# GpSimd's inverse square roots of the norms, issued in pieces of two columns

## The chip, the cores and the metric

One Trainium2 chip, of which the kernel uses one core. The metric is device time in microseconds (us) of one execution; less is better. The engines of the core are named as the profile names them: PE (TensorE, with PEld for its weight loads), DVE (VectorE), ACT (ScalarE), POOL (GpSimd), and SP, which issues most DMAs.

## The reference

One layer of a hybrid block on 512 tokens of width 1024, in float32: a norm and one wide projection `z = h @ w_in`, three token mixers fed from `z` (HGRN2, RWKV-7, multi-head latent attention), a gated merge, an output projection, and a gated feed-forward. The change touches the places where an inverse square root is taken:

```python
def rms_norm(x, g):                                   # in and out of both halves, HGRN2's heads, the two MLA ranks
    y = xf * lax.rsqrt(jnp.mean(xf * xf, axis=-1, keepdims=True) + NORM_EPS)
...
kk = heads(k * k_k)                                   # RWKV-7: unit-length keys, 16 heads
kk = kk * lax.rsqrt(jnp.maximum(jnp.sum(kk * kk, axis=-1, keepdims=True), 1e-24))
...
y = ((y - mean) * lax.rsqrt(var + RW_LNX_EPS))        # RWKV-7: norm of each head's output
```

## The kernel before

Tokens or features lie on the 128 partitions. Products that need full precision are made of three passes over operands split into a high and a low part (`mm3`, lines 137 to 139: high by high, low by high, high by low). The wide projections are streamed: `stream` (line 209 on) takes a slab of weights (DMA, then ACT makes the high part at line 205, then DVE the low part at line 132) and issues groups of three matmuls of 512 columns into a PSUM tile named mmD. Everything else of the mixers is interleaved between these groups on PE: the preparation of RWKV's eight pairs of heads (`rwkv_prep`), its chain over eight chunks (`rwkv_chain`), HGRN2's eight heads (`hgrn_head`), and the attention (`mla_low` and what follows). The order on each engine is made by the tile framework's scheduler, which plans by priorities ("lanes") and by its own simulated timeline, so a change in how many instructions an engine gets moves work on all engines.

The dense groups are paced by POOL. After the last matmul of each paced group POOL writes one element (the tile token, line 149, `pace`), and the first matmul of a group waits for the token of the group five places earlier. There are 912 tokens, one for each paced group, all on POOL's queue in order. The streams of the feed-forward are not paced.

POOL also does the powers: `power_mhalf` (line 277) raises a tile of sums to -0.5 by one `tensor_tensor` with `op=pow` against a constant tile filled with -0.5. It is called on these tiles:

- nrs, one column, eight times, and rrs, one column, eight times (`to_fm` and `project`, by way of `rstd`): the norms over the width of 1024.
- rs, eight columns, once for each of RWKV's eight pairs (line 552). Its input ss (line 550) is made by DVE from the sums of squares that four small products (line 547) leave in PSUM. ACT then copies rs broadcast into a tile (line 555, named t), and PE transposes it (line 557).
- hrs, four columns, once for each of HGRN2's eight heads (line 899). ACT reads it column by column (line 901).
- lnr, sixteen columns, four times, once for each two chunks of the chain (line 788). DVE reads it at line 789.
- mrs, eight columns, once (line 1011), from the sums of products at line 1001. DVE reads the first four columns (line 1013), PE the other four, one at a time, as weights (line 1016).

Of the kernel before, what the change touches and what calls it, by code (L numbers as in the profile page):

```python
# [17 lines left out]
ALU = mybir.AluOpType  # L18
# [84 lines left out]
class Kern:  # L103
# [172 lines left out]

    def power_mhalf(self, dst, src):
        p, n = src.shape
        self.nc.gpsimd.tensor_tensor(dst, src, self.mhalf[:p, :n], op=ALU.pow)  # L279

    def vec(self, name, j):
        o = VOFF[name] + j
# [1083 lines left out]
```

## Time and profile before

| what | value |
|---|---|
| time, median of 3 runs | 1403.33 us (1401.97 to 1404.83) |
| time of the profiled execution | 1408.42 us |
| its span, first to last instruction | 1406.6 us |
| mean granted TensorE clock | 0.996 |
| instructions in the span | 27356 |
| PE busy | 1354.8 us (96%) |
| PEld busy | 1103.2 us (78%) |
| DVE busy | 848.3 us (60%) |
| ACT busy | 638.6 us (45%) |
| POOL busy | 190.8 us (14%) |

A busy share is the time in which the engine had an instruction under way. Matmuls overlap in the pipeline, so one matmul's duration is longer than the distance to the next. In a timeline each row has the start, the length of the merged stretch, the engine, the line, the operation, output<-input and the count, and in brackets how long the engine sat idle before it and what ended that wait.

### The profile page before, as it was taken

Reading aid. Unit: us, or ns where it says so; the run is one execution under the profiler, and the core shown is the slowest. Engines: PE = TensorE matmul, PEld = TensorE weight load, DVE = VectorE, ACT = ScalarE, POOL = GpSimd, SP = SyncE. Lnnn points to the kernel's source line nnn. Section 1 sums busy time; section 2 is a strip of 40 time slices with the busy share of each in tenths; the row PEclk is TensorE's granted clock in tenths of the full one; section 3 lists DMA queues with packets and bytes.
Section 4 is the critical chain, followed back from the end, with each engine's and each line's share of the span. In section 5 each row is a group of like instructions: output and inputs, shape, how many; then the busy total and the mean of one; then the engine's idle time right before and its main releaser. Section 6 shows DMA issues by size and latency. Waiting matters only on the chain.

```text
span 1406.6 us, 27356 instructions
## 1 busy us (share of the span) xinstructions
PE 1354.8 (96%) x9664; PEld 1103.2 (78%) x9664; DVE 848.3 (60%) x1756; ACT 638.6 (45%) x1259; POOL 190.8 (14%) x1042
## 2 busy tenths in 40 slices
PE   6999999999999999999999999999999999999998
PEld 5777777777777777888788888877888888888886
DVE  5567797797787784575665576655575344343234
ACT  5554546556556453433665354443354333332222
POOL 2122132131222311242210000001010000000000
PEclk9999999999999999999999999999999999999999
DMA  5565467557755777986464555415544333334233
GB/s 180 149 193 144 129 183 227 178 153 218 213 157 155 242 237 227 356 277 208 137 204 147 157 178 168 130 53 173 198 139 135 98 97 92 102 95 156 97 98 105
DMA packets 196025, 231.62 MB, mean 165 GB/s; under 512 B 42672, under 2 KB 137392, under 8 KB 195888
## 3 DMA queue, kind: packets, MB, share of 16 engines
q1 hardware_dynamic: 194496, 226.72, 52.1%
q10 hardware_dynamic: 1392, 3.15, 0.7%
q8 instruction: 76, 1.25, 0.4%
q14 instruction: 61, 0.50, 0.1%
HBM read 169.65 MB, written 60.16 MB: 163 GB/s over the span
## 4 chain that ended last, share of the span: by engine, by line
PE 82%; DMA 6%; DVE 4%; issue 4%; ACT 3%; POOL 1%; SPq 1%; POOLq 0%; DVEq 0%; ACTq 0%
PE mmD L137 18%; PE mmD L138 17%; PE mmD L139 17%; PE po L137 4%; PE po L139 4%; PE po L138 4%; PE pr L194 1%; DMA wsD<-in_w_in_dram 1%; DMA z<-zst 1%; DMA zr<-z 1%; PE pmo L1138 1%; PE pm L137 1%; PE pm L139 1%; PE pm L138 1%; PE ph L843 1%
## 5 line engine op out<-in xcount | busy, mean ns | idle before, releaser
L137 PE MATMUL mmD<-xH,whD 128*128 128x512 f32 (+1 forms) x1232 | 486.2, 397 | 11.9 <-POOL token L149 5.6
L138 PE MATMUL mmD<-xL,whD 128*128 128x512 f32 (+1 forms) x1232 | 474.2, 386 | 0.0
L139 PE MATMUL mmD<-xH,wlD 128*128 128x512 f32 (+1 forms) x1232 | 469.6, 385 | 0.9 <-DVE wlD L132 0.9
L132 DVE TENSOR_TENSOR wlD<-wsD,whD 128x512 fp32r<-128x512 f32 x384 | 263.2, 687 | 292.0 <-ACT whD L205 276.0
L205 ACT CAST whD<-wsD 128x512 fp32r<-128x512 f32 x384 | 236.7, 618 | 375.8 <-PE mmD L138 244.1
L137 PEld LDWEIGHTS mmD<-xH,whD 128*128 128x128 f32 x1232 | 232.0, 189 | 65.2 <-POOL token L149 8.9
L139 PEld LDWEIGHTS mmD<-xH,wlD 128*128 128x128 f32 x1232 | 232.2, 189 | 48.6 <-DVE wlD L132 2.0
L138 PEld LDWEIGHTS mmD<-xL,whD 128*128 128x128 f32 x1232 | 233.5, 190 | 40.1
L149 POOL MEMSET token<- 1x1 f32 x912 | 82.2, 90 | 675.4 <-PE mmD L139 660.1
L139 PE MATMUL po<-whD,fL 128*128 128x512 f32 x176 | 68.6, 390 | 0.0
L138 PE MATMUL po<-wlD,fH 128*128 128x512 f32 x176 | 68.6, 390 | 0.0
L137 PE MATMUL po<-whD,fH 128*128 128x512 f32 x176 | 61.9, 390 | 0.0
L279 POOL TENSOR_TENSOR rrs<-rtm,mhalf 128x1 f32<-128x1 f32 x8 | 4.4, 551 | 402.3 <-DVE rtm L274 368.7
L646 DVE TENSOR_TENSOR invtmp<-inv 64x30 f32<-64x30 f32 (+14 forms) x120 | 38.7, 322 | 17.7 <-DMA inv<-Ld 16.0
L594 POOL TENSOR_SCALAR BK<-BK,gC 128x128 f32<-128x128 f32 x56 | 47.0, 854 | 11.8 <-PE pr L194 11.8
L237 ACT COPY zst<-mmD 128x512 f32<-128x512 f32 x64 | 37.3, 583 | 14.6 <-PE mmD L139 14.4
L647 DVE TENSOR_TENSOR inv<-inv,invtmp 64x30 f32<-64x30 f32 (+14 forms) x120 | 38.4, 320 | 2.2
L139 PEld LDWEIGHTS po<-whD,fL 128*128 128x128 f32 x176 | 33.0, 188 | 7.0
L138 PEld LDWEIGHTS po<-wlD,fH 128*128 128x128 f32 x176 | 33.0, 188 | 7.0
L137 PEld LDWEIGHTS po<-whD,fH 128*128 128x128 f32 x176 | 33.0, 188 | 7.0
L843 PEld LDWEIGHTS ph<-hq,hk 128*32 128x32 f32 x1536 | 17.6, 111 | 18.0 <-issue 9.6
L1136 ACT COPY mpT<-pmt 128x128 f32<-128x128 f32 (+3 forms) x32 | 13.6, 425 | 38.0 <-PE pmt L1134 37.9
(349 smaller groups left out, 1960.1 us busy)
## 6 DMA issues: line engine op xcount, KB each, us to landing
wsD<-in_w_in_dram SPq DMA_DIRECT2D x176, 256.0 KB, 3.4
wsD<-in_w_ffn_in_dram SPq DMA_DIRECT2D x96, 256.0 KB, 2.8
z<-zst SPq DMA_DIRECT2D x63, 256.0 KB, 3.3
rwd<-G SPq DMA_DIRECT2D x28, 512.0 KB, 5.5
G<-rwd SPq DMA_DIRECT2D x28, 512.0 KB, 6.7
wsD<-in_w_branch_dram SPq DMA_DIRECT2D x48, 256.0 KB, 2.9
wsD<-in_w_ffn_out_dram SPq DMA_DIRECT2D x44, 256.0 KB, 2.6
zr<-z SPq DMA_DIRECT2D x26, 256.0 KB, 3.3
```

Of the source, the lines that this page charges most:

```text
L132: (eng or self.nc.vector).tensor_tensor(dst, src, high.bitcast(F32), op=ALU.subtract)
L137: first = mm(ps, lhsT=lh, rhs=rh, start=start, stop=False)
L138: mm(ps, lhsT=lh, rhs=rl, start=False, stop=False)
L139: return first, mm(ps, lhsT=ll, rhs=rh, start=False, stop=stop)
L149: token = self.nc.gpsimd.memset(self.token, 0.0).ins
L194: last = c()
L205: nc.scalar.copy(h, st)
L237: self.nc.scalar.copy(st[:m], ps)
L594: Pl.tensor_scalar(BK[:, c], BK[:, c], gC[:, c + 1:c + 2], None, op0=ALU.mult)
L646: V.tensor_tensor(tv, cv, rv, op=ALU.mult)
L647: V.tensor_tensor(U[:, :j, j + 1:], U[:, :j, j + 1:], tv, op=ALU.add)
L843: mm(g[b:b + HB, o // P, :], lhsT=k[:, t], rhs=q[:, t], start=True, stop=True)
```

## The change

`power_mhalf` issues one power for each two columns in place of one for the whole tile. Nothing else is edited; lines behind it move by three.

```diff
     def power_mhalf(self, dst, src):
         p, n = src.shape
-        self.nc.gpsimd.tensor_tensor(dst, src, self.mhalf[:p, :n], op=ALU.pow)
+
+        for c in range(0, n, 2):
+            m = slice(c, min(c + 2, n))
+            self.nc.gpsimd.tensor_tensor(dst[:, m], src[:, m], self.mhalf[:p, m], op=ALU.pow)
```

A tile of one column keeps its one instruction. rs and mrs become four instructions each, hrs two, lnr eight. The scheduler's order moves with it on every engine.

On POOL at the fifth pair of RWKV's preparation (lw is the pair's decay tile, rs the powers, token the pacing of the dense groups, BK the scaled keys), before:

```order
L521 MEMSET lw_5663 128x8
L149 MEMSET token 1x1 x8
L279 TENSOR_TENSOR rs_5691<-ss_5689,mhalf 128x8
L149 MEMSET token 1x1 x24
L594 TENSOR_SCALAR BK_5702<-BK_5702,gC_4658 128x128 x4
```

and the same place in the changed kernel:

```order
L524 MEMSET lw_5675 128x8
L149 MEMSET token 1x1 x5
L282 TENSOR_TENSOR rs_5703<-ss_5701,mhalf 128x2 x3
L149 MEMSET token 1x1
L282 TENSOR_TENSOR rs_5703<-ss_5701,mhalf 128x2
L149 MEMSET token 1x1 x31
```

The power is now four instructions, with one token between the third and the fourth. Counted from the start of the queue, 284 tokens stand ahead of the first piece, where 282 stood ahead of the whole power.

On POOL at the end of the chain and the start of the attention (krL is a zeroed half of a tile, mrs the attention's powers, lnr the chain's last powers), before:

```order
L1039 MEMSET krL_10418 64x512
L149 MEMSET token 1x1 x10
L279 TENSOR_TENSOR mrs_10377<-mtm_10376,mhalf 128x8
L279 TENSOR_TENSOR lnr_7451<-lnv_7450,mhalf 128x16
L149 MEMSET token 1x1 x270
```

and in the changed kernel:

```order
L1042 MEMSET krL_10481 64x512
L149 MEMSET token 1x1 x9
L282 TENSOR_TENSOR lnr_7496<-lnv_7495,mhalf 128x2 x8
L282 TENSOR_TENSOR mrs_10437<-mtm_10436,mhalf 128x2 x4
L149 MEMSET token 1x1 x254
```

The two powers have changed places: all eight pieces of lnr stand ahead of mrs, and no token stands between.

On PE at the same place, the products that read mrs (line 1016 before, 1019 now) among the dense groups, before:

```order
L137 MATMUL mmD_4155<-xH_10_111,whD_4181 128x512
L138 MATMUL mmD_4155<-xL_18_119,whD_4181 128x512
L139 MATMUL mmD_4155<-xH_10_111,wlD_4182 128x512
L137 MATMUL mmD_4156<-xH_9_110,whD_4181 128x512
L138 MATMUL mmD_4156<-xL_17_118,whD_4181 128x512
L139 MATMUL mmD_4156<-xH_9_110,wlD_4182 128x512
L1016 MATMUL pm_10385<-cst,mrs_10377 128x128 x4
L1028 MATMUL pm_10398<-cst,msq_10396 128x64 x4
L137 MATMUL mmD_4156<-xH_10_111,whD_4181 128x512
```

and in the changed kernel:

```order
L137 MATMUL mmD_4252<-xH_9_110,whD_4277 128x512
L138 MATMUL mmD_4252<-xL_17_118,whD_4277 128x512
L139 MATMUL mmD_4252<-xH_9_110,wlD_4278 128x512
L765 MATMUL yb_7531<-cst,y_6655 128x128
L765 MATMUL zus_7542<-cst,y_6655 128x128
L1019 MATMUL pm_10448<-cst,mrs_10437 128x128 x2
L1031 MATMUL pm_10461<-cst,msq_10459 128x64 x4
L1019 MATMUL pm_10448<-cst,mrs_10437 128x128 x2
L137 MATMUL mmD_4252<-xH_10_111,whD_4277 128x512
```

Between the last product at line 1001 (now 1004) and the first that reads mrs stand seven dense groups before and five now; the four products that read mrs are now two and two.

## The prediction

> **What bounds the kernel now.** I read the page first, then the stretches, then the powers' own line, and last the timelines of POOL and PE around the powers. The page's first part, and two stretches (busy us of each engine, then clock, DMA share, GB/s):
>
> ```profile
> PE 1354.8 (96%) x9664; PEld 1103.2 (78%) x9664; DVE 848.3 (60%) x1756; ACT 638.6 (45%) x1259; POOL 190.8 (14%) x1042
> ```
>
> ```profile
> 30.00:460.00 430.00, 410.95 (x3383) 321.06 (x3384) 324.50 (x721) 240.32 (x479) 99.11 (x497) 1.00 0.59 175
> 460.00:700.00 240.00, 232.88 (x2857) 187.75 (x2855) 153.82 (x329) 104.49 (x214) 55.65 (x237) 0.99 0.74 242
> ```
>
> PE is the bound all along. In the stretch where RWKV and HGRN2 are mixed into the dense groups (30 to 700 us) it is idle for 19.1 + 7.1 = 26.2 us. A slower POOL costs time only where PE ends up waiting, and it can wait in two ways: for a token that is queued behind a power, or for a copy or product that reads the power. Both are there already (waiter, what ended the wait, us in total, times, longest):
>
> ```profile
> PE mmD L137 <- POOL token L149: 5.6, 6, 1.8
> PE pr L557 <- ACT t L555: 2.6, 2, 1.6
> ```
>
> **What a piece costs.** The powers by width (durations min/median/max in ns, first and last start):
>
> ```profile
> L279 POOL TENSOR_TENSOR nrs<-ntm,mhalf x8: 548/549/555, 5.9 to 1037.5; 128x1 f32<-128x1 f32 x8
> L279 POOL TENSOR_TENSOR rs<-ss,mhalf x8: 1644/1668/2534, 57.0 to 458.7; 128x8 f32<-128x8 f32 x8
> L279 POOL TENSOR_TENSOR hrs<-htm,mhalf x8: 1008/1062/1400, 185.7 to 661.9; 128x4 f32<-128x4 f32 x8
> L279 POOL TENSOR_TENSOR lnr<-lnv,mhalf x4: 2899/2900/2900, 597.7 to 686.0; 128x16 f32<-128x16 f32 x4
> L279 POOL TENSOR_TENSOR mrs<-mtm,mhalf x1: 1639/1639/1639, 684.4 to 684.4; 128x8 f32<-128x8 f32 x1
> ```
>
> From 8 to 16 columns it is (2900 - 1644)/8 = 157 ns a column, and 1644 - 8 x 157 = 388 ns are left as the fixed part (1 column by this: 545, the row has 549; 4 columns: 1016, the row has 1008). Two columns are 388 + 314 = 0.70 us. No row has a power of two columns, nor two small powers back to back, so the distance between pieces is bounded: from below by the columns alone, 0.31 us, from above by 0.70. The nearest pair of rows are the two powers at the end of the chain, on POOL (start, length):
>
> ```profile
> 684.35 1.64 POOL L279 TENSOR_TENSOR mrs<-mtm,mhalf 128x8 f32<-128x8 f32 x1 [1.45 <-DVE lnv L274]
> 685.96 2.90 POOL L279 TENSOR_TENSOR lnr<-lnv,mhalf 128x16 f32<-128x16 f32 x1
> 688.80 0.67 POOL L149 MEMSET token<- 1x1 f32 x5
> ```
>
> The second starts 1.61 us after the first, which is 1.64 long: 0.03 of overlap, so the fixed part is paid each time. I take 0.67 for each piece and 0.70 for the last. The Trainium skill speaks against this in its "GPSIMD Engine Reference", section "Instruction dispatch": completion gates whoever waits for an instruction's semaphore, and does not hold back the next Pool instruction. Pieces without waits between them could by that rule hide each other's fixed cost, and the four pieces of rs would take what one power takes. The pair above shows 0.03 us of such hiding.
>
> So rs and mrs go from 1.64 to 2.71 us (+1.07), hrs from 1.01 to 1.37 (+0.36), lnr from 2.90 to 5.39 (+2.49); the sixteen powers of one column stay as they are. POOL gets 8 x 1.07 + 1.07 + 8 x 0.36 + 4 x 2.49 = 22.5 us more. It is 14% busy, so this by itself is nothing; what counts is where it delays PE.
>
> **Term 1, RWKV's eight pairs (rs).** Behind a power the tokens are queued; the group five places on waits for each, at the head of PE's queue, with everything else of PE behind it. POOL and PE at the second and the fifth pair, and PE alone at the sixth and the seventh:
>
> ```profile
> 110.87 1.67 POOL L279 TENSOR_TENSOR rs<-ss,mhalf 128x8 f32<-128x8 f32 x1 [2.11 <-DVE ss L550]
> 112.49 0.53 POOL L149 MEMSET token<- 1x1 f32 x4
> ...
> 281.99 1.80 POOL L279 TENSOR_TENSOR rs<-ss,mhalf 128x8 f32<-128x8 f32 x1 [4.88 <-DVE ss L550]
> 283.74 0.67 POOL L149 MEMSET token<- 1x1 f32 x5
> ```
>
> ```profile
> 112.64 0.50 PE L137 MATMUL mmD<-xH,whD 128*128 128x512 f32 x1 [0.65 <-POOL token L149]
> ...
> 283.88 0.51 PE L137 MATMUL mmD<-xH,whD 128*128 128x512 f32 x1 [1.77 <-POOL token L149]
> ...
> 344.56 0.66 PE L557 MATMUL pr<-cst,t 128*128 128x128 f32 x4 [0.96 <-ACT t L555]
> ...
> 401.64 0.66 PE L557 MATMUL pr<-cst,t 128*128 128x128 f32 x4 [1.60 <-ACT t L555]
> ```
>
> The tokens come in a burst right behind the power, and PE starts 0.15 us after the first of them: no slack at all. If the order stayed, nearly every pair would cost the whole +1.07, some 8 us. But the scheduler's order moves too. I counted PE's work between the products that feed rs (line 547) and the dense group that waits for the first token behind the power, from the order, with a dense group at 0.69 us:
>
> ```profile
> 690.04 0.09 POOL L149 MEMSET token<- 1x1 f32 x1 [0.56 <-PE mmD L139]
> 690.73 0.09 POOL L149 MEMSET token<- 1x1 f32 x1 [0.60 <-PE mmD L139]
> ```
>
> (tokens of groups that follow each other start 0.69 apart.) That cover stays the same at the first, second and eighth pair; it grows by 1.1, 1.5 and 1.6 us at the third, fourth and fifth (at the fifth the shown rows have two more tokens ahead of the pieces); it shrinks by 0.4 and 1.1 at the sixth and seventh, where on the other hand the transposes that wait now stand 2 to 2.7 us later. So: pairs 1, 2 and 8, +0.9 each; pairs 3, 4 and 5, -0.9 together, since they can win no more than they wait today; pairs 6 and 7, +0.8 together. Sum +2.6 (at most +8 if the longer cover does not help).
>
> **Term 2, the end of the chain (lnr, then mrs).** Here PE waits today, as the rows of PE show, from about 687.6 to 688.94, behind mrs and lnr in this order:
>
> ```profile
> 686.05 1.16 PE L1016 MATMUL pm<-cst,mrs 128*128 128x128 f32 x8
> 687.14 0.46 PE L1028 MATMUL pm<-cst,msq 64*128 64x64 f32 x4
> 688.94 0.51 PE L137 MATMUL mmD<-xH,whD 128*128 128x512 f32 x1 [1.35 <-POOL token L149]
> ```
>
> The chain of waits has the last products ahead of mrs, and DVE's rows tell when the two inputs are ready:
>
> ```profile
> 680.15 0.79 PE pm L1001 x8
> ```
>
> ```profile
> 684.04 0.23 DVE L1010 TENSOR_SCALAR mtm<-mtm 128x4 f32<-128x4 f32 x2
> 684.18 0.17 DVE L274 TENSOR_SCALAR lnv<-lnv 128x16 f32<-128x16 f32 x1
> ```
>
> Both are ready at about 684.3, 3.4 us after the products end at 680.94. In the changed order PE has five dense groups and two transposes in between, some 3.7 us, and then stands at the products that read mrs. POOL starts at the same 3.4, takes 5.39 for lnr and 3 x 0.67 for the mrs pieces that the first two products need: ready at 10.8. PE waits 7.1 us where it waits 1.35 now: +5.8. If lnr's input comes up to 1.5 us ahead of mrs's, the wait is as much shorter, +4.3. I take +5.2.
>
> **Term 3, the rest.** At the first three lnr PE has room: tokens were written at 600.57, and the group that waits for the first of them, by count, starts at 604.05 behind the chain's own products:
>
> ```profile
> 600.57 0.53 POOL L149 MEMSET token<- 1x1 f32 x4
> ```
>
> ```profile
> 604.05 0.50 PE L137 MATMUL mmD<-xH,whD 128*128 128x512 f32 x1
> ```
>
> 3.4 us of slack against +2.49: nothing, +0.2 each for safety (up to +2.49 each if that slack is other waiting that goes). The eight hrs add 0.36 where no slack is left, at two of the eight, less up to 0.3 us each since ACT can start on the first two columns after 0.70 in place of 1.01: 0 to +1.2 for all, +0.6 taken.
>
> Sum: 2.6 + 5.2 + 0.6 + 0.6 = 9.0. A stall of PE lets DMA, ACT and DVE get ahead, which shortens some of the 18 us that PE waits in this stretch for other things (26.2 less 5.6 and 2.6): a sixth of the stall, my estimate, 1.5. That leaves +7.5 us. The profiled execution's 1408.42 (span 1406.6 and 1.8 around it) would be 1415.9; it lies 5.1 above the median of the runs, so against the median of 1403.33 the forecast is **1410.8 us**.
>
> **The rivals.** *No change: the pieces overlap.* Each piece follows the last after its columns' time alone, the lower bound of 0.31. POOL's powers are then as long as before and only the order acts: pairs 3 to 7 lose perhaps 4 us of waits, the swapped powers at the chain's end wait 3.4 + 2.90 + 1.3 - 3.7 = 3.9 in place of 1.35, +2.5. Sum -1.5: 1401.8. For it: no semaphore stands between the pieces. Against it: the 0.03 us. Chance 0.13, with other ways to end within noise. (This is where the Trainium skill's section on instruction dispatch would lead.)
>
> *Faster: the new order hides the powers.* Mechanism: the transposes of pairs 5 to 7 stand later, so the waits of 1.77, 0.96 and 1.60 go (-4.3), HGRN2's ACT starts 0.3 us earlier at eight heads (-2.4), pairs 1, 2 and 8 cost +2.7, and at the chain's end lnr's input comes at least 5.8 us ahead of mrs's, so its term is nought; from there on the change gains. Sum -4.0: 1399.3. For it: the longer cover counted above. Against: both inputs were ready together. Chance 0.12.
>
> *Much slower: no cover holds.* The cover at pairs 3 to 5 is eaten by an input that comes later as well (+8), two of the first three lnr stall in full (+5), the chain's end costs +5.8: +19 before give-back, +16: 1419. For it: DVE's queue sets when ss comes, and there it idles POOL 4.88 us at the fifth pair. Chance 0.13.
>
> **Numbers.** The forecast's own case (+3 to +12) has 0.62. The range is 1402.0 to 1418.0: it leaves out the faster case and half of the much slower one. A measurement of this kernel tells 0.2%, 2.8 us, from no change. Faster 0.12, within 0.2% 0.13, slower 0.75.
>
> **What would show it.** In the changed trace: pieces of rs 0.67 apart on POOL, not 0.31; lnr 5.4 us long in all; PE's wait at the products that read mrs near 7 us; its waits for tokens up from 5.6 us; waits at pairs 3 to 5 not up. The forecast is wrong if a piece follows in under 0.45 us, if lnr is done before mrs's input is ready, or if PE's idle time elsewhere falls by as much as it grows here.

## The result, and the profile after

The changed kernel takes 1427.42 us (median of 4 runs, 1422.98 to 1429.37) where before takes 1404.08 us (4 runs, 1401.97 to 1405.75): a ratio of 1.0163, 95% interval 1.0132 to 1.0193. It is slower, by some 23 us where 7.5 were forecast. The profiled execution took 1429.05 us with a span of 1427.3 us, 20.7 more than the span of before. The first part of its page, and the mean granted clock, which was 0.996 in before:

```profile
PE 1363.7 (96%) x9664; PEld 1107.5 (78%) x9664; DVE 848.4 (59%) x1756; ACT 639.8 (45%) x1259; POOL 220.6 (15%) x1105
```

```profile
core 0: 1427.3 us, clock 0.989
```

POOL is busy 29.8 us more (22.5 were forecast). PE is busy 8.9 us more for the same work, most of which is the clock, as shown below. The two stretches that the prediction quoted:

```profile
30.00:460.00 430.00, 403.62 (x3258) 314.63 (x3257) 317.81 (x704) 229.01 (x452) 110.68 (x520) 1.00 0.59 173
460.00:700.00 240.00, 233.25 (x2904) 186.07 (x2903) 147.28 (x316) 104.18 (x221) 63.99 (x256) 0.97 0.73 241
```

In the first stretch PE is idle for 26.4 us in place of 19.1, and it gets through 3258 matmuls in place of 3383. The powers of each tile (busy us, mean ns of one, POOL's idle time before them), and then two of the rs on POOL (start, length of all four pieces):

```profile
L282 POOL TENSOR_TENSOR rs<-ss,mhalf 128x2 f32<-128x2 f32 x32 | 25.1, 812 | 24.8 <-DVE ss L553 24.8
L282 POOL TENSOR_TENSOR lnr<-lnv,mhalf 128x2 f32<-128x2 f32 x32 | 23.6, 768 | 14.5 <-DVE lnv L274 10.5 <-DVE mtm L1013 4.0
L282 POOL TENSOR_TENSOR hrs<-htm,mhalf 128x2 f32<-128x2 f32 x16 | 13.7, 874 | 9.7 <-DVE htm L274 9.6
```

```profile
109.59 2.79 POOL L282 TENSOR_TENSOR rs<-ss,mhalf 128x2 f32<-128x2 f32 x4 [2.09 <-DVE ss L553]
167.24 3.87 POOL L282 TENSOR_TENSOR rs<-ss,mhalf 128x2 f32<-128x2 f32 x4 [5.47 <-DVE ss L553]
```

Four pieces take 2.79 us at the second pair, 0.70 each, so next to nothing overlaps. At the third pair the same four take 3.87. What PE waits for (us in total, times, longest):

```profile
PE mmD L137 <- POOL token L149: 10.1, 13, 1.8
PE yb L765 <- DVE y L792: 7.0, 1, 7.0
PE mmD L137 <- ACT zst L237: 6.1, 7, 2.0
PE pr L550 <- ACT t L546: 4.3, 3, 2.9
```

and two rows of before that the prediction does not show:

```profile
PE mmD L137 <- ACT zst L237: 2.9, 2, 2.2
PE pr L547 <- ACT t L543: 1.2, 2, 0.9
```

Waits for tokens rise from 5.6 to 10.1 us. Two waits that have nothing to do with powers rise as well: that of dense groups for zst (ACT's copy that empties an earlier group's PSUM tile) from 2.9 to 6.1, and that of the products that feed rs for their operand t (the squares, line 543 before and 546 now) from 1.2 to 4.3. The readers of rs (line 557 before, 560 now), which waited 2.6, wait no more. And there is a new wait of 7.0 us, at the end of the chain. The rows of DVE, POOL and PE there:

```profile
707.70 0.17 DVE L274 TENSOR_SCALAR lnv<-lnv 128x16 f32<-128x16 f32 x1
707.77 0.23 DVE L1013 TENSOR_SCALAR mtm<-mtm 128x4 f32<-128x4 f32 x2
...
713.76 1.23 DVE L792 TENSOR_TENSOR y<-y,lnr 128x1024 f32<-128x1024 f32 x1 [5.15 <-POOL lnr L282]
```

```profile
707.94 5.79 POOL L282 TENSOR_TENSOR lnr<-lnv,mhalf 128x2 f32<-128x2 f32 x8 [4.03 <-DVE mtm L1013]
713.69 3.15 POOL L282 TENSOR_TENSOR mrs<-mtm,mhalf 128x2 f32<-128x2 f32 x4
```

```profile
707.65 0.39 PE L139 MATMUL mmD<-xH,wlD 128*128 128x512 f32 x1
715.05 0.47 PE L765 MATMUL yb<-cst,y 128*128 128x128 f32 x1 [7.00 <-DVE y L792]
716.25 1.22 PE L1019 MATMUL pm<-cst,mrs 128*128 128x128 f32 x4 [0.51 <-POOL mrs L282]
...
718.88 0.77 PE L137 MATMUL mmD<-xH,whD 128*128 128x512 f32 x1
719.46 0.63 PE L138 MATMUL mmD<-xL,whD 128*128 128x512 f32 x1
```

The eight pieces of the last lnr run from 707.94 to 713.73, DVE normalises y with them, and only then can PE transpose y (line 765). After 7 us without work PE's matmuls of 512 columns last 0.63 us in place of 0.39. The stretches show why (length, busy us of PE, PEld, DVE, ACT and POOL, then the granted clock, the DMA share and GB/s):

```profile
709.50:712.90 3.40, 0.00 (x0) 0.00 (x0) 0.00 (x0) 0.00 (x0) 3.40 (x6) 1.00 0.29 77
712.90:716.30 3.40, 0.74 (x3) 0.34 (x3) 1.40 (x2) 0.74 (x1) 3.40 (x6) 0.51 0.00 0
716.30:719.70 3.40, 3.40 (x14) 2.96 (x15) 2.27 (x6) 2.83 (x6) 0.94 (x6) 0.50 0.00 0
719.70:723.10 3.40, 3.40 (x9) 2.63 (x9) 3.40 (x8) 1.66 (x3) 0.18 (x2) 0.50 0.21 77
723.10:726.50 3.40, 3.40 (x20) 2.86 (x20) 1.93 (x4) 2.03 (x4) 0.36 (x4) 0.99 0.52 154
```

For 10.2 us, from 712.9 to 723.1, the clock is half, and PE has work in 7.6 of them. Up to the last matmul, half clock lies over 27.3 us in place of 10.2, and PE works in 24.7 of them in place of 10.2. Matmuls of 512 columns that follow each other start 0.43 us apart there and 0.23 at full clock, so about half of this working time is lost: 12.3 us in place of 5.1, which is +7.2. PE is idle up to the last matmul for 56.6 us in place of 44.8, which is +11.8. Together that is 19.0 of the 20.7 us by which the span grew.

### The profile page after: what moved, and what is told of

Read it like the earlier page. It is cut to its first block, busy times and chain, and to the rows that moved or that the text cites. A ratio compares the mean times of both kernels' runs of the same rounds, so it can differ in the third digit from the quotient of the medians.

```text
span 1427.3 us, 27412 instructions
## 1 busy us (share of the span) xinstructions
PE 1363.7 (96%) x9664; PEld 1107.5 (78%) x9664; DVE 848.4 (59%) x1756; ACT 639.8 (45%) x1259; POOL 220.6 (15%) x1105
## 4 chain that ended last, share of the span: by engine, by line
PE 79%; DMA 7%; DVE 4%; issue 3%; POOL 3%; ACT 3%; SPq 1%; POOLq 0%; DVEq 0%; ACTq 0%
PE mmD L137 18%; PE mmD L138 17%; PE mmD L139 17%; PE po L137 4%; PE po L138 4%; PE po L139 4%; DMA wsD<-in_w_in_dram 1%; PE pr L194 1%; POOL rs L282 1%; DMA rvd<-lw 1%; PE pm L137 1%; PE pm L138 1%; PE pm L139 1%; PE pmo L1141 1%; PE yb L194 1%
## 5 line engine op out<-in xcount | busy, mean ns | idle before, releaser
L137 PE MATMUL mmD<-xH,whD 128*128 128x512 f32 (+1 forms) x1232 | 488.6, 399 | 18.1 <-POOL token L149 10.1
L282 POOL TENSOR_TENSOR rs<-ss,mhalf 128x2 f32<-128x2 f32 x32 | 25.1, 812 | 24.8 <-DVE ss L553 24.8
```

The source lines that it names most:

```text
L137: first = mm(ps, lhsT=lh, rhs=rh, start=start, stop=False)
L282: self.nc.gpsimd.tensor_tensor(dst[:, m], src[:, m], self.mhalf[:p, m], op=ALU.pow)
```

## The experiments

**The chain's end.** Four edits leave the order of everything ahead of it as in the changed kernel. The first issues mrs at the highest priority, so that it goes ahead of lnr:

```diff
+        cur = self.cur_lane
+        self.lane(0)
         self.power_mhalf(rs, tm)
+        self.lane(cur)
```

> The changed kernel with one edit: mrs's power gets the tokens' priority, so its four pieces stand behind two of lnr's, and the transposes of the chain's last output (which read lnr's result) no longer stand ahead of the products that read mrs on PE. Theory 'transposes': PE lost its 7.0 us because those transposes stood at the head of its queue; with them out of the way 6 to 10 us come back, 1417 to 1421. Theory 'block': POOL's block of twelve pieces (8.9 us) holds back the tokens behind it whatever stands first, so PE only waits at another instruction; 1 to 2.5 us come back, 1425 to 1426.5.

Measured, as a ratio to before like all that follow: 1.0123 (1.0086 to 1.0160). The wait moved to the products that read mrs, and 2.3 us of waiting for a token came behind it:

```profile
PE pm L1022 <- POOL mrs L282: 3.8, 1, 3.8
```

The second gives PE six products of 512 columns, which nobody reads, after lnr's first piece:

```diff
+        if last:
+            d = self.t(self.pC, [P, S], "zus")
+            for i in range(6):
+                nc.tensor.matmul(d[:2], lhsT=rs[:, :2], rhs=sq.rearrange("t n c -> t (n c)")[:, :S], start=True, stop=True)
```

> The changed kernel with six products of 512 columns added on PE that need only the first piece of the last lnr (their result is never read), so PE has work in part of its 7.0 us wait. Theory 'clock': part of the loss is the half clock granted from 712.9 us on for 10.2 us, because PE had stood still; with PE busy the clock stays and 3 to 5 us come back, 1422 to 1424.5. Rival 'wait alone': the half clock costs nothing that counts; no change or the length of the products that overhang, 1427 to 1429.

Measured: 1.0124 (1.0092 to 1.0156). The stretch of the wait keeps its full clock (1.00, the third number from the end):

```profile
690.00:720.00 30.00, 26.81 (x154) 18.05 (x154) 15.17 (x32) 16.58 (x29) 10.44 (x31) 1.00 0.32 99
```

The third puts the last lnr and mrs behind five more tokens:

```diff
+        with self.tc.issue_after(self.token_ins[662]) if last else ExitStack():
+            self.rstd(rs, m2, C, LNX_EPS, m2)
...
+        with self.tc.issue_after(self.token_ins[662]):
+            self.power_mhalf(rs, tm)
```

> The changed kernel with the last lnr and mrs put behind five more tokens on POOL, tokens whose groups are done before the pieces start. The transposes that read lnr's result still stand early on PE. Theory 'block': PE gets five more groups to run and 3 to 6 us come back, 1421.5 to 1424.5. Theory 'transposes': PE stands at them as before; 0 to 1 us, 1426.5 to 1427.5.

Measured: 1.0108 (1.0074 to 1.0142). The fourth puts the transposes of line 765 behind more dense groups as well:

```diff
+            with self.tc.issue_after(self.last_ins[667]):
+                for i in range(NT):
+                    nc.tensor.transpose(pt[:, i * P:(i + 1) * P], y[:, i, p].rearrange("t e d -> t (e d)"), self.ident)
```

> The last experiment's order of POOL, and on PE the transposes held behind the five groups that those tokens release. If the loss at the chain's end is a wait that needs both the tokens and the transposes out of the way, both theories give 6 to 9 us back here, 1418 to 1421.5, and more than either alone. If the 11.6 us were only the place where an earlier delay shows, nothing comes back: 1426 to 1428.

Measured: 1.0119 (1.0077 to 1.0162). In these two the transposes still wait for y, 3.7 and 3.0 us in place of 7.0:

```profile
PE yb L766 <- DVE y L794: 3.7, 1, 3.7
```

```profile
PE yb L768 <- DVE y L796: 3.0, 1, 3.0
```

All four ratios lie some 0.4% under the 1.63% of the change, but each interval overlaps that of the changed kernel. They also share one set of runs of before, with a median of 1407.48 us where the change's own round had 1404.08; in plain time the four are 0.9 to 3.3 us under the changed kernel. So these runs make it likely, and do not show, that the chain's end is a part of the loss. None of them takes the whole of it away either: in the first, third and fourth PE still waits 3.0 to 3.8 us there at one instruction, and half clock lies over 6.8 to 10.2 us near it.

**Parts of the change.** From here two theories stand against each other: P, the price (POOL is longer at the powers, and tokens and readers are late by it), and O, the order (the scheduler makes a new order of all engines' instructions, and before's was better). The edit chooses which tiles go in pieces (three runs in one cut, with the conditions of the second and the third behind the first):

```diff
-        for c in range(0, n, 2):
+        step = 2 if dst.name.startswith('rs') else n     # e5;  n == 4: e6;  n == 16: e7
+        for c in range(0, n, step):
```

and the last takes `range(0, n, 4)` for all.

> Only the eight rs are issued in pieces of two columns; lnr, hrs and mrs are whole as before. Theory P (the price: each piece costs POOL 0.67 us and what is queued or waits behind it is late by the difference): 8 x 1.07 us with little cover is +4 to +9 us, all of it before 600 us of the trace, and at the end of the chain a wait near the one of before (1.4 us); ratio to before 1.003 to 1.007. Theory O (the order: any change in the number of POOL's instructions makes the scheduler plan anew, and before's order is a good one by luck): +8 to +12 us whatever the pieces cost, ratio 1.006 to 1.009, and the same for the run with only hrs in pieces.

> Only the eight hrs are issued in pieces of two columns: 8 x 0.36 = 2.9 us more on POOL, the smallest price of the four tiles with more than one power, but a new order on every engine. Theory P: 0 to +2 us, ratio 1.000 to 1.0015. Theory O: as much as with only rs in pieces, +8 to +12 us, ratio 1.006 to 1.009.

> Only the four lnr are issued in pieces (eight each); rs, hrs and mrs are whole. The order on PE is nearly that of before, and at the end of the chain mrs stays ahead of lnr. Theory P: 4 x 2.49 us on POOL, some of it covered at the first three; at the last one the token behind it is late by 2.49: +3 to +8 us, ratio 1.002 to 1.006, with PE waiting for a token some 3.8 us at the end of the chain. Theory O: the order hardly moves, so only the last wait grows: +2.5 us, ratio 1.002.

> All powers in pieces of four columns: a piece is 388 + 4 x 157 = 1.0 us, so rs and mrs are 2.0 us (+0.36), lnr 4.05 (+1.15), hrs as before: 9 x 0.36 + 4 x 1.15 = 7.8 us more on POOL where pieces of two add 22.5. mrs stays ahead of lnr at the end of the chain. Theory P: about a third of the change's loss, +2 to +7 us, ratio 1.0015 to 1.005. Theory O: +8 to +12 us like any other order, ratio 1.006 to 1.009.

Measured: rs alone 1.0129 (1.0101 to 1.0157); hrs alone 1.0027 (1.0015 to 1.0040); lnr alone 1.0048 (1.0028 to 1.0067); pieces of four columns 1.0077 (1.0053 to 1.0100). P holds for lnr alone and O for pieces of four. For the other two neither holds. rs alone costs nearly twice the most that P gave it, and more than O gave it; its waits for tokens alone rise by 9.5 us:

```profile
PE mmD L137 <- POOL token L149: 15.1, 13, 2.4
```

hrs alone, with a new order and 3.4 us more on POOL, costs 0.27%: less than O says and more than P does.

**Cover and order.** Two runs put the tokens eight groups ahead in place of five (`PACE = 8`), with whole powers and with pieces; with eight, three more groups stand between a token and the group that waits for it. A third has ACT's copy of rs in four pieces, so that each transpose needs one piece. The fourth keeps before and adds two copies of one column to each rs, for a new order at little price. The three edits:

```diff
-PACE = 5
+PACE = 8
```

```diff
-        A.copy(rb, rs.unsqueeze(2).to_broadcast([P, 2 * NT, C]))
+        for i in range(NT):
+            h = slice(2 * i, 2 * i + 2)
+            A.copy(rb[:, h], rs[:, h].unsqueeze(2).to_broadcast([P, 2, C]))
```

```diff
+        cur = self.cur_lane
+        self.lane(0)
+        for i in range(2):
+            self.nc.gpsimd.tensor_copy(self.t(rt, [P, 1], "rs2"), ss[:, i:i + 1])
+        self.lane(cur)
```

> Before, with whole powers, but the first matmul of a group waits for the token of the group eight places earlier in place of five; the order changes on every engine. Theory P (the price: what is queued or waits behind a power is late): with whole powers the token waits of 5.6 us fall to some 1 us, -4 to 0 us, ratio 0.997 to 1.000. Theory O (the order: before's order is a good one by luck, any other loses): +4 to +12 us, ratio 1.003 to 1.009.

> The changed kernel, with the first matmul of a group waiting for the token eight places earlier: three groups more, some 2.1 us of cover, which is twice the 1.07 us that the pieces add at an rs. Theory P: the token waits of 10.1 us fall to some 2 us, the rest (readers of rs and mrs, the chain's end) stays: ratio to before 1.008 to 1.012, and 1.008 to 1.012 to the run of before with eight as well. Theory O: ratio near that of the run of before with eight, since both have an order other than before's, and the pieces add little: within 0.4% of each other.

> The changed kernel, with ACT's copy of rs in four pieces of two heads too, so that the first transpose waits for one piece of the power and one of the copy. It has four ACT copies of 128 columns in place of one of 512 (0.62 us). Theory P: the wait of the transposes for the copy (4.3 us in all) goes, the tokens' stays: ratio to before 1.010 to 1.014. Theory O: an order other than that of the changed kernel, ratio anywhere from 1.006 to 1.016. If the readers' lateness is the main cost: 1.005 to 1.010.

> Before, with whole powers, and two POOL copies of one column with each rs, one ahead of it and one behind the first token, whose output nobody reads. They cost POOL little (an element or a column takes 0.1 to 0.3 us on this engine in the trace of before), yet the scheduler's order changes on every engine, about as much as in the changed kernel. Theory P: 8 x 0.1 to 0.3 us, +1 to +3 us, ratio 1.0005 to 1.002. Theory O: +8 to +12 us, ratio 1.006 to 1.009. Between these (1.002 to 1.005), an order by itself costs about as much as hrs alone in pieces (1.0027), and the rest of the 1.0163 is price.

Measured: before with eight 1.0051 (1.0022 to 1.0080), where P had expected no loss and O this size; pieces with eight 1.0096 (1.0075 to 1.0117); copies in pieces 1.0151 (1.0125 to 1.0177), which gains nothing beyond the noise; the control 1.0046 (1.0030 to 1.0062). With eight ahead and pieces, tokens are all but gone as a wait, and the readers of rs wait:

```profile
PE pr L560 <- ACT t L558: 4.0, 1, 4.0
...
PE mmD L137 <- POOL token L149: 0.5, 1, 0.5
```

The control's copies cost 0.30 us each, 4.8 us for all 16, so that its 0.46% (6.5 us) is order and price in a proportion that this run does not tell:

```profile
L556 POOL COPY rs<-ss 128x1 f32<-128x1 f32 x16 | 4.8, 302 | 23.4 <-DVE ss L550 23.4
```

**Eight ahead only where RWKV is.** Before with eight was a few us ahead of before at the chain's end, by the work that PE had done, and lost more than that behind it. So these runs take eight (or six) for the first 640 groups and five from there, with whole powers, with pieces, and with only rs in pieces:

```diff
-        if len(self.tokens) >= PACE:
-            self.tc.add_manual_dep(first.ins, self.tokens[-PACE], dep, reason="pace")
+        ahead = 8 if len(self.tokens) < 640 else PACE
+        if len(self.tokens) >= ahead:
+            self.tc.add_manual_dep(first.ins, self.tokens[-ahead], dep, reason="pace")
```

> Before, whole powers, with the tokens eight places ahead for the first 640 groups (up to the chain's end) and five from there. In the trace of before with eight ahead throughout, PE was 4.3 us ahead of before at the chain's end and lost 10.6 us behind it. If these two are separable: -4 to 0 us, ratio 0.997 to 1.000, faster than both kernels. If any new order costs its 0.3 to 0.5% (theory O): 1.003 to 1.005.

> The changed kernel with the tokens eight places ahead for the first 640 groups and five from there. Theory P, tokens: most of the pieces' price upstream is gone, what is left is the readers' and the chain's end: 1.004 to 1.009, and 0.3 to 0.6% over the same pacing with whole powers. If the readers of rs, hrs and lnr are the main cost: over 1.010. Theory O: within 0.3% of the same pacing with whole powers.

> Only rs in pieces, with the tokens eight places ahead for the first 640 groups. Only rs in pieces with five ahead had a ratio of 1.0129. If held tokens are the main cost of rs in pieces: within 0.2 to 0.4% of the same pacing with whole powers, 1.000 to 1.005. If its readers (ACT's copy, the transposes) are: 1.008 to 1.013.

> Before, whole powers, with the tokens six places ahead for the first 640 groups: a second control of the order, with 0.7 us more cover behind each power. Cover alone: -3 to 0 us, ratio 0.998 to 1.000. Theory O: 1.003 to 1.005 as in the other runs with whole powers and a new order.

Measured: whole with eight 1.0093 (1.0077 to 1.0109); pieces with eight 1.0101 (1.0074 to 1.0127); only rs with eight 1.0113 (1.0099 to 1.0127); whole with six 1.0116 (1.0101 to 1.0131). All four lie above what was expected if waits for tokens were the main cost, and the two with whole powers lie above what O gave them too. No version beats before: whole powers with fewer token waits cost 0.9 and 1.2%. With six ahead, the waits for tokens are down to 2.6 us from 5.6, and those for zst are up to 7.7 from 2.9:

```profile
PE mmD L137 <- ACT zst L238: 7.7, 7, 2.6
...
PE mmD L137 <- POOL token L150: 2.6, 4, 1.4
```

With eight ahead, pieces come out 0.1 to 0.45% over whole powers (1.0101 against 1.0093, 1.0113 against 1.0093, 1.0096 against 1.0051), with intervals that overlap in all three, against 1.63% with five. And whole powers in another order, with another pacing, can cost most of what the change costs (1.16%). So price and order have to be parted with the order held.

**The order held.** The last two runs chain each engine's instructions with edges that fix only the order of issue: the pieces in the order of before, and the whole powers in the order of the changed kernel (`line` is an engine's instructions in the wanted order, with the pieces of one power next to each other). The traces show the wanted order on all engines.

```diff
+            for a, b in zip(line, line[1:]):
+                self.tc.add_manual_dep(b, a.name, dep, reason="order")
```

> The changed kernel, all powers in pieces of two, with every engine's instructions held in the order of before (the pieces stand together where the whole power stood). Theory P (price): the prediction's own reckoning for an order that stays: nearly every rs costs its +1.07 us at the tokens, 8 us, hrs up to 1.2, and at the chain's end the token waits for mrs and lnr that are 1.07 + 2.49 us longer, +3.6: +9 to +14 us, ratio 1.006 to 1.010. Theory O (order): the price is hidden, 0 to +4 us, ratio 1.000 to 1.003. By both in equal parts: 1.005 to 1.008.

> Before, with whole powers, with every engine's instructions held in the order of the changed kernel (the whole power stands where its first piece stood). Theory P: the order is neutral, POOL's powers as short as before; at the chain's end the wait behind lnr and mrs is 3.4 + 2.90 + 1.64 less the 3.7 of work in front, some 4 us in place of 1.35: 0 to +4 us, ratio 1.000 to 1.003. Theory O: the order carries most of the loss: +12 to +20 us, ratio 1.009 to 1.014. By both in equal parts: 1.005 to 1.009.

Measured: pieces in the old order 1.0112 (1.0092 to 1.0132); whole powers in the new order 1.0064 (1.0039 to 1.0090). One of the second's seven runs took 7518 us; it is left out, and no cause for it is known. The product of the two ratios is 1.0177, within the interval of the change itself: **price 1.12%, some 15.8 us, and order 0.64%, some 9.0 us, account for the change within the noise.** Each theory has a part of it: the price is a little above what P gave it, and the order lies between what P and O gave it. The three profiled executions agree less well: the spans of these two grew by 13.9 and 12.2 us, 26.1 together, where the change's grew by 20.7. The profiled execution of the whole powers is the longest of its six runs (1412.2 to 1420.6 us).

The clock and PE's waits with pieces in the old order (its line numbers are others; line 668 is the transposes that read the copy of rs, before's line 557), then two places on POOL, the seventh pair and the chain's end, and PE at the chain's end:

```profile
core 0: 1420.5 us, clock 0.994
```

```profile
PE mmD L224 <- POOL token L236: 16.3, 10, 4.1
...
PE pr L668 <- ACT t L666: 7.0, 2, 4.0
...
PE mmD L224 <- ACT zst L324: 3.1, 3, 1.3
```

```profile
404.19 4.89 POOL L369 TENSOR_TENSOR rs<-ss,mhalf 128x2 f32<-128x2 f32 x4 [3.38 <-DVE ss L661]
...
693.17 2.72 POOL L369 TENSOR_TENSOR mrs<-mtm,mhalf 128x2 f32<-128x2 f32 x4 [1.38 <-DVE mtm L1121]
695.86 5.24 POOL L369 TENSOR_TENSOR lnr<-lnv,mhalf 128x2 f32<-128x2 f32 x8
```

```profile
701.20 0.75 PE L224 MATMUL mmD<-xH,whD 128*128 128x512 f32 x1 [4.14 <-POOL token L236]
```

The price is where P has it: +10.7 us of waits for tokens, +4.4 at the readers of rs, +0.7 by half clock, and nearly nothing at zst (+0.2). The span grew by 13.9, so a few other waits are shorter. At the chain's end the wait for the token is 4.14 us in place of 1.35. The clock and PE's waits with whole powers in the new order (line 653 is the products that feed rs, before's line 547), and POOL at the chain's end:

```profile
core 0: 1418.8 us, clock 0.991
```

```profile
PE mmD L224 <- ACT zst L324: 8.1, 8, 2.0
...
PE yb L868 <- DVE y L895: 4.7, 1, 4.7
PE pr L653 <- ACT t L649: 3.3, 2, 3.0
PE mmD L224 <- POOL token L236: 2.8, 4, 1.4
```

```profile
702.32 3.44 POOL L366 TENSOR_TENSOR lnr<-lnv,mhalf 128x16 f32<-128x16 f32 x1 [4.04 <-DVE mtm L1116]
705.72 1.64 POOL L366 TENSOR_TENSOR mrs<-mtm,mhalf 128x8 f32<-128x8 f32 x1
```

The new order takes 2.8 us of waits for tokens away, and all 2.6 of the readers', and brings 5.2 at zst, 4.7 at the transposes of y and 2.1 at the products that feed rs. Half clock lies over 20.5 us in place of 10.2 up to the last matmul, with PE at work in 19.3 of them, which is 4.6 more. The sum of these, 11.2, is all but 1 us of the 12.2 by which the span grew.

## Why the prediction was wrong

The side was right and the size was not: 1410.8 us was forecast, with a range to 1418.0, and 1427.4 was measured. The step that failed is the sum's account of what the new order does. It counted only waits that a power ends, let the waits for everything else shrink (the give-back of 1.5), and had no term for the clock. In the trace of the changed kernel the waits for everything else grew, and half clock, which stood at nothing, cost some 7.2 us more than in before.

**What a piece costs** was right where POOL has its operands to itself: 0.70 us, with no more overlap than the 0.03 of the prediction's pair of powers. This also ends the rival by which pieces hide each other, the one to which the Trainium skill's "GPSIMD Engine Reference", section "Instruction dispatch", would have led: no semaphore stands between the pieces, and still the next one starts no sooner. The price was too small beside DVE. The seventh pair's whole power took 2.53 us in before, as the row of rs with its maximum of 2534 ns said in the prediction's own fence, and its four pieces take 4.89 in the same order. DVE's rows in that time, some of which follow, are mostly TENSOR_TENSORs one after the other, and each piece meets some of them:

```profile
404.54 0.67 DVE L959 TENSOR_TENSOR hq<-hq,hf 128x512 f32<-128x512 f32 x1
405.14 0.38 DVE L757 TENSOR_TENSOR invtmp<-inv 64x228 f32<-64x228 f32 x1
405.56 0.39 DVE L758 TENSOR_TENSOR inv<-inv,invtmp 64x228 f32<-64x228 f32 x1
```

The Trainium skill has this in "SBUF — State Buffer", section "SBUF: two separate sides": a DVE instruction with two SBUF inputs and a GpSimd instruction that reads SBUF shut each other out for a whole instruction. The traces agree. A piece lasts 0.70 alone and 1.22 on average here. Over all twenty traces, the 359 pieces of two columns that meet no DVE instruction with both inputs in SBUF last 0.68 to 0.72 us, and 64 of these run beside other DVE instructions, with one input or with one in PSUM. Of the 509 that do meet one, 233 last over 0.8 us, and the longest 2.39. So POOL's +22.5 us was +29.8. The prediction's 8 us for an order that stays, with 3.6 at the chain's end and up to 1.2 at hrs as the expectation of the run with pieces in the old order adds them, are 12.8; that run measured 15.8. This term was mis-sized by nearly a quarter.

**Term 1's count** held, and its cover failed elsewhere. In the changed kernel pairs 1, 2 and 8 wait 3.1 us more for tokens (2.7 forecast), pairs 3 to 5 wait 0.7 less (0.9 forecast), and pairs 6 and 7, tokens and readers together, 0.2 less (0.8 more was forecast): +2.2 where +2.6 stood. The second pair, which waited 0.65 in before:

```profile
112.47 0.50 PE L137 MATMUL mmD<-xH,whD 128*128 128x512 f32 x1 [1.75 <-POOL token L149]
```

Whole powers in the new order wait 4.0 us less at tokens and readers ahead of the chain's end than before does, so the longer cover is there. But the prediction counted only waits that a power ends. In the new order the waits for zst rise by 3.2 us and those of the products that feed rs by 3.1, and both rise with whole powers too, and hardly with pieces in the old order, so they come with the order. It is as if the work that moved in between had covered ACT where it stood before; no run moved it back to show that. By the terms of the prediction the new order was worth some 4 us: 12.8 of price became 9.0 ahead of the give-back. It costs some 9. This swing of 13 us is most of the 16 that are missing.

**Term 2, the chain's end,** had the right length of idle time at the wrong instruction. It counted the two transposes of line 765 among the work that covers, though they read y, which DVE normalises with lnr; they are the ones that wait. The waits of 7.0 and 0.51 us in place of 1.35 are +6.2, where +5.2 stood. What the sum did not have at all is the half clock behind this wait, 10.2 us long, in which PE works for 7.6; that costs up to 3.8 more.

**Term 3** was right for lnr: at the first three lnr the trace has one wait for a token, of 0.2 us. For hrs the runs do not part price from order: hrs alone costs 0.27%, some 4 us, where 0.6 stood. **The give-back** of 1.5 was not there: in the stretch from 30 to 700 us PE waits 23 us for other things than tokens and readers of rs, where it waited 18. **The rival "much slower"** came nearest in time (1419), by a mechanism that was not the one: the covers held, and other inputs came late. **The rival "faster"** had a part of the order's mechanism, which took waits at the powers away as it said, and had nothing of what the order brings.

Of what was to show the forecast right, three signs came true: pieces of rs stand 0.67 apart where DVE leaves them alone, PE waits 7 us at the chain's end (though at the transposes), and the waits for tokens are up. The last lnr took 5.79 us beside DVE where 5.4 were expected. One sign failed: waits at pairs 3 to 5 are up after all, since the products that feed rs wait up to 2.9 us there.

What stays open is why orders with whole powers cost between 0.5 and 1.2%. Their traces show waits at zst, at t and at y, but no run gave one of these back by itself. They have more half clock in common: 17.1 to 37.5 us in place of 10.2. In the control PE is idle for 3.1 us less than in before, and the span is 5.7 us longer all the same, with half clock over 23.9 us. Nor did any run hold before's own order with whole powers, so a cost of the ordering edges themselves, if there is one, is in both the price and the order.

## What to carry to other kernels

Where a scheduler makes the order, a change of instructions is two changes, its price and a new order. Hold the order fixed in one run and the price in another, and the two can be read apart. Work that moves to cover one wait may leave another uncovered, so count cover at every input that the engine waits for, ACT's and DVE's too, and not only at those that the edit touches, and look at the clock behind each long wait. Splitting this power on GpSimd paid its fixed part again each time, and gave DVE one more chance to shut it out.

## What was not expected of the hardware

In these traces PE's clock halves after much less than a whole idle window. The twenty traces of this study can be cut into the windows of 3.41 us in which the clock changes; counted are windows at full clock past the first 20 us, up to the last matmul. Of 60 in which PE was idle for 1.8 us or more, 58 were followed by half clock; of 72 with 1.4 to 1.8 us of idle time, 22; of 7862 with less, 28, so idle time is not the whole of it. Each window at half clock costs up to 1.7 us on top of the wait, if PE has work all through. The Trainium skill's "TensorE: Matmul & The Clock Gate", Part 1, has the window (3413 ns, free-running), with which these traces agree, and lets the clock fall after an idle one; here half an idle one was enough. Since the windows run freely, the same wait can cost it in one run and not in another, which may be a part of the runs' spread of a few us; no run here shows that.
